# A's scores scaled and reduced by one VectorE operation, and an order computed with a shared port

## The chip, the cores and the metric

The kernel runs on one core of a Trainium2 chip. The metric is the device time of one execution in microseconds (us), and the median of several executions where more are there. TensorE is PE in the profile (its weight loads are PEld), VectorE is DVE, ScalarE is ACT, GpSimd is POOL, and SyncE, which issues most DMAs, is SP.

## The reference

Two layers over 512 latent tokens and 256 context tokens of width 1024. Each layer normalises and modulates its input, projects it once, and attends in three groups of eight heads of 64:

```python
hx = rmsnorm(x, norm_w) * (1 + scale[:, None, :]) + shift[:, None, :]
px = split_cols(hx @ w_in); pc = split_cols(hc @ w_in)
ya, yca = global_gqa(...)            # A: every latent query reads all 512 latent and 256 context keys
yb, ycb = neighbourhood_attn(...)    # B: a window of 8 x 16 grid cells with a learned bias, and all context keys
yc_, ycc = window_gqa(...)           # C: +-128 tokens with a sink logit, and all context keys
ux = jnp.concatenate([ya, yb, yc_], axis=-1) * jax.nn.silu(px[9])
x = x + gate[:, None, :] * (ux @ w_out)
```

In A, queries and keys are RMS-normalised per head before the rotary turn, so a row of A's scores carries a factor that belongs to its query: `softmax(r * s)`, with one `r` for each query and head. The context tokens attend to the context alone, in the first layer only. A final RMSNorm ends the kernel.

## The kernel before

Everything is float32, and each product is taken as three products of rounded halves (`hh`, `hl`, `wh`, `wl`), which is why TensorE has so much to do. The attention of a layer goes by pairs of heads: four pairs of B, then A and C in turn (A0, C0, A1, C1, ..., A3, C3). While one pair attends, TensorE also projects q, k, v and gates of pairs to come; under the last pair (C3) it starts the output projection instead (`head`, L512), and the projected rows that this reads are reloaded and split just ahead of use (`reload`, `split_u`, L484 and L485).

A pair is cut into units. A unit of A (`GlobalUnit`) is one head and two tiles of 128 queries; its scores, 768 columns a tile, fill the three PSUM banks of `Sbig`, so tile 0 ends and tile 1 begins in the middle bank. A `CtxUnit` (layer 0) is the 256 context queries of one head, 256 columns for each of two tiles. For each tile of A three steps follow: VectorE takes the negated maximum of the raw scores out of PSUM (L1167), multiplies it by `r` (L1169, one element a row), and ScalarE computes `exp(r * s - max)` from PSUM into a tile `P` in SBUF, with `r` as its scale (L1171). A DMA on SP's queue then copies `P` to a tile `R5` or `R2`, shown as R (`ship`, L1052), so that `P` may be used anew; there are two buffers of `P`, for all units of A, B and C. TensorE turns R into a bank `T` (L1057), ScalarE rounds it to `pth` (L785), VectorE keeps the rest in `ptl` (L1037), and TensorE multiplies both with the values into `Obig` (L1041). Units of C and B do it otherwise: one VectorE operation adds a mask or bias to the scores, writes them to `P` in SBUF, and finds their extreme (L1219, L1279, a `tensor_tensor_reduce`; the trace calls it CUSTOM_DVE_ANT_0, the order ISA), and ScalarE's exponential works in place on `P` (L1222, L1281).

What sets the order is `arrange`: once the program is written, a model of the five engines, the DMA queues and the buffers (`Step.cost`, `Graph.run`) plays it several times with ranks from the pass before, and the best order is fixed, engine by engine, by added dependencies. Engines run their instructions strictly in that order. [...] So a change of one cost can move instructions anywhere.

Of the kernel before, what the change touches and what calls it, by code (L numbers as in the profile page):

```python
# [12 lines left out]
F32 = mybir.dt.float32  # L13
F32R = mybir.dt.float32r
BF16 = mybir.dt.bfloat16
AF = mybir.ActivationFunctionType
OP = mybir.AluOpType
AX = mybir.AxisListType
# [32 lines left out]
CFG = dict(hp=600, hpf=600, pj=2, T=2, O=1, P=2, R5=5, R2=2, qt=5, kt=4, vt=4, gt=3, wh=5, ws=3, pt=3, bm=2, tA=1, OT=1, u=1, tl=1, turns=6, ab="pj", tR=1, map={}, ada=2, h0=300, h1=1000, a0=9, H=2, hr=0, cp="A", cv="A", w0="D", w1="D", w2=(("D", "D"), ("D", "D")), hb="D", ws_="P")  # L51
# [14 lines left out]
def body(tc, xT, small, bcast, rpb, adaw, adat, wt, wf, wo, trigA, trigQ, trigC, mskB, mskC, outT):  # L66
    nc = tc.nc
    es = ExitStack()
    const = es.enter_context(tc.tile_pool(name="const", bufs=1))
# [6 lines left out]
    ident = const.tile([128, 128], F32)  # L76
# [8 lines left out]
    nc.vector.memset(ones, 1.0)  # L85
    mhalf = const.tile([128, 8], F32)
    nc.vector.memset(mhalf, -0.5)
    onesw = const.tile([128, 64], F32)
    nc.vector.memset(onesw, 1.0)
    onepair = const.tile([128, 2], F32)  # L90
    nc.vector.memset(onepair, 0.0)
    for h in range(2):
# [363 lines left out]
    udram = {}  # L456
# [302 lines left out]
def mixers(tc, nc, l, last, p1, ps, const, env):  # L759
    g_ = env  # L760
    en = g_["en"]
    (pj, Sbig, psT, psO, half_O, opv, after, ADA, wlo, proj_f, proj_t, ada, ada_load, ident, identr, bc, sm, pairs, onesw, mhalf, negsink, udram, dram, hpool, rpb,
     trigA, trigQ, trigC, mskB, mskC) = [g_[k] for k in (
         "pj", "Sbig", "psT", "psO", "half_O", "opv", "after", "ADA", "wlo", "proj_f", "proj_t", "ada", "ada_load", "ident", "identr", "bc", "sm", "pairs", "onesw", "mhalf",
         "negsink", "udram", "dram", "hpool", "rpb", "trigA", "trigQ", "trigC", "mskB", "mskC")]
    nq = 4 if last else 6
    ncol = nq * 128
# [335 lines left out]
    def ahead(steps):  # L1103
# [10 lines left out]
        late[0](late[1])  # L1114
        yield late[2]

    class CtxUnit(Unit):
        def scores(self):
            S = Sbig[:, 0:512]
            for t in range(2):  # L1120
                for x in range(2):
                    mul(S[:, t * 256:(t + 1) * 256], self.Q[:, NT + t * 128:NT + (t + 1) * 128],
                                     self.K[:, x, NT:NA], start=(t == 0 and x == 0), stop=(x == 1),
                                     skip_group_check=True)
            nm = self.stat("negm", 4, 2)
            nc.vector.tensor_reduce(nm, S[:, 0:512].rearrange("p (t c) -> p t c", t=2), axis=AX.X, op=OP.max,
                                    negate=True)
            if self.sink is not None:
                nc.vector.tensor_scalar(nm, nm, self.sink, None, op0=OP.min)
            rs = self.c["rs"]  # L1130
            if rs is not None:
                nc.vector.tensor_mul(nm, nm, rs[:, 4:6, self.h])
            P = newP()
            for t in range(2):
                nc.scalar.activation(P[:, t * 256:(t + 1) * 256], S[:, t * 256:(t + 1) * 256], AF.Exp,
                                     bias=self.stat("negm", 4 + t), accum_out=self.stat("sums", 4 + t),
                                     **({} if rs is None else dict(scale=rs[:, 4 + t, self.h:self.h + 1])))
            self.P = ship(P, 512)
            yield 0.45

# [13 lines left out]
    class GlobalUnit(Unit):  # L1154
        def scores(self):
            self.P = []
            for i in self.tiles:
                cx, loc = ((512, 0), (768, 1024))[i % 2]
                for c0, c1, o in ((NT, NA, cx), (0, NT, loc)):
                    for x in range(2):  # L1160
                        mul(Sbig[:, o:o + c1 - c0], self.Q[:, i * 128:(i + 1) * 128],
                                         self.K[:, x, c0:c1], start=(x == 0), stop=(x == 1), skip_group_check=True)
                yield 0.65
            for i in self.tiles:
                S = Sbig[:, 768 * (i % 2):768 * (i % 2) + 768]
                nm = self.stat("negm", i)
                nc.vector.tensor_reduce(nm, S, axis=AX.X, op=OP.max, negate=True)  # L1167
                r = self.c["rs"][:, i, self.h:self.h + 1]
                nc.vector.tensor_mul(nm, nm, r)  # L1169
                P = newP()  # L1170
                nc.scalar.activation(P, S, AF.Exp, bias=nm, scale=r, accum_out=self.stat("sums", i))  # L1171
                self.P.append(ship(P, 768, ((512, 768), (0, 256))[i % 2]))
                yield 0

# [403 lines left out]
    def urgent(gen):  # L1578
        while True:
# [10 lines left out]
ENGINES = {"PE": "PE", "Activation": "ACT", "DVE": "DVE", "Pool": "POOL", "SP": "SP"}  # L1590
CAPS = dict(x0=8, ada=9, x1=8, sq=3, rstd=3, pj=CFG["pj"], ws=CFG["ws"], wh=CFG["wh"], wl=CFG["wh"], hL=16, hC=16,
            T=CFG["T"], spr=2, nw=1, P=CFG["P"], R5=CFG["R5"], R2=CFG["R2"], qt=CFG["qt"], kt=CFG["kt"], vt=CFG["vt"], gt=CFG["gt"], negm=2,
            bm=CFG["bm"], sums=2, pth=CFG["pt"], ptl=CFG["pt"], rec=2, ssA=2, qd=2, rs=3, ex=2, xr=3, xn0=8, room=9,
            xn1=8, rbl=2)
POOLS = ("p0_", "p1_0_", "p2_0_", "p1_1_", "p2_1_")
BANKS = ("pj", "T", "Sbig", "Obig")
# [11 lines left out]
def size(ap):  # L1608
    n = 1
    for _, c in ap[1:]:  # L1610
        n *= c
    return n


class Step:
# [16 lines left out]
    def cost(self, tiles):  # L1632
        ins = [u for u in self.use if not u[1]]
        outs = [u for u in self.use if u[1]]
        n = max([size(u[2]) for u in ins + outs[:1]] or [0])
        bank = any(stem(u[0].name) in BANKS for u in ins)
        op = str(getattr(self.inst, "op", getattr(self.inst, "func", ""))).split(".")[-1]
        e = self.engine
        self.plain, self.turn, self.switch = False, None, 0.0
        if self.dma:  # L1640
            b = 4 * outs[0][2][0][1] * size(outs[0][2])
            out = stem(outs[0][0].name).split("_")[0]
            far = any(u[0].name not in tiles or tiles[u[0].name][1] for u in ins)
            self.busy = ISSUE.get(out, 430.0)
            self.fixed = 2400.0 if far else 1650.0
            self.move = 3460.0 if out == "bc" else b / (340.0 if far else 395.0)
        elif e == "PE":
            n = size(ins[0][2])
            exact = ins[0][4] == "float32"
            self.turn = outs[0][0].name if stem(ins[0][0].name) in ("ident", "identr") and n == 128 else None  # L1650
            self.switch = 5.0 if exact else 86.0
            self.busy = {128: 108.0, 256: 57.0, 2: 112.0}[n] if exact else n / 2.4 + (13.5 if n > 128 else 12.0)
            self.last = 272.0 if exact else n / 2.4 + 180.0
        else:
            if e == "ACT":
                d = 172.0 + 0.83 * n + (0 if bank else 35)
            elif e == "DVE":
                d = 156.0 + 0.52 * n if self.kind == "InstTensorCopy" and not bank else 152.0 + 1.06 * n
                self.plain = self.kind == "InstTensorTensor" and not bank and n >= 256
            elif op == "pow":  # L1660
                d = 1000.0
            elif self.kind == "InstTensorScalarPtr":
                d = 440.0 + 2.2 * n if n > 8 else 190.0
            else:
                d = 190.0 + 2.14 * n if n > 64 else 150.0
            self.busy = max(d - BEHIND[e], 20.0)
            self.last = d
            if e == "ACT" and op == "Exp" and n > 12:
                self.busy, self.last = d - 16, d + 91
# [18 lines left out]
class Graph:  # L1688
# [76 lines left out]
    def run(self, rank):  # L1765
# [14 lines left out]
        for t, v in self.order.items():  # L1780
            if self.pool[t] is not None:
                stage_left[self.pool[t]] += len(v)
        lanes, ring, data = [], {}, {}
        prev, row, done = None, 0, 0

        def push(k):
# [10 lines left out]
        while done < n:  # L1797
# [42 lines left out]
            if s.dma:  # L1840
                begin = max(t + s.fixed, ring.get(e, 0.0))
                fin = begin + s.move
                for x, (a, b) in data.items():
                    if x != e:
                        fin += 0.5 * max(0.0, min(b, fin) - max(a, begin))
                ring[e], data[e] = fin, (fin - s.move, fin)
                lanes.append(fin)
                fin += TO_LAND
            elif e == "PE":
                fin = t + s.last  # L1850
                if not s.turn and prev is not None and prev.turn:
                    busy += prev.switch
                    fin += prev.switch
                row = row + 1 if s.turn else 0
                if row > 2 and s.switch > 5:
                    busy += 20
                if t < SLOW:
                    busy *= 2
                    fin += s.last
                prev = s  # L1860
            else:
                extra = 0.55 * min(free["POOL"] - t, s.last) if s.plain and free["POOL"] > t else 0.0
                fin = t + s.last + extra
                busy += extra
            free[e] = t + busy
# [194 lines left out]
```

## Time and profile before

| | |
|---|---|
| three executions | 1184.32, 1188.16, 1190.93 us; median 1188.16 |
| the profiled execution | 1184.9 us, span 1183.1 us, granted TensorE clock 0.989 |
| PE | busy 1121.9 us, 95% of the span (ends of matmuls are modelled) |
| DVE, ACT, POOL | 789.7 us (67%), 689.4 us (58%), 409.8 us (35%) |
| attention of A and C | about 240 to 600 us in layer 0, about 840 to 1125 us in layer 1 |

A row of a group names line, engine, operation, tiles and shapes, the count, then busy time and mean time of one. A row of waits names who waited for whom, the total in us, how often, and the longest. In a timeline, the bracket is the idle time of the engine before the row and what ended it. In a table of stretches, the last three columns are the granted TensorE clock, the share of DMA time and GB/s.

### The profile page before, as it was taken

How to read it: one execution, taken by the hardware profiler on the slowest of the kernel's cores; microseconds unless marked ns; L12 is line 12 of the kernel's file. 1: busy time of each engine (PE TensorE's matmuls, PEld its weight loads, DVE VectorE, ACT ScalarE, POOL GpSimd, SP SyncE). 2: the span in 40 equal slices, each digit the busy share in tenths (PEclk: the TensorE clock that was granted, in tenths of full speed). 3: DMA queues.
4: the chain of work that ended last, by engine and by line, in shares of the span. 5: the costliest groups of instructions: out<-in, count | busy, mean ns of one | idle time of the engine just before them, and what ended most of it. 6: DMA issues, size and time to landing. Idle time of an engine off the chain costs nothing. (4 is left out here: it accounts for less than half of the span.)

```text
span 1183.1 us, 21230 instructions
## 1 busy us (share of the span) xinstructions
PE 1121.9 (95%) x7352; PEld 977.3 (83%) x7352; DVE 789.7 (67%) x1548; ACT 689.4 (58%) x1466; POOL 409.8 (35%) x364
## 2 busy tenths in 40 slices
PE   5999899999999999998789999999999999999996
PEld 3798888997878888887678989988987888887776
DVE  6666667655565668669879765678557566758653
ACT  5445555565666667777632544565566677677551
POOL 2430202155454365536200012121166655475001
PEclk9999999999999999999899999999999999999998
DMA  9555435435465455456758542565344444566352
GB/s 344 182 165 163 148 124 189 147 126 160 154 194 169 155 176 187 134 173 212 215 175 318 176 152 78 166 195 170 110 157 161 157 165 166 169 182 203 133 170 72
DMA packets 111540, 200.95 MB, mean 170 GB/s; under 512 B 13676, under 2 KB 32456, under 8 KB 111432
## 3 DMA queue, kind: packets, MB, share of 16 engines
q1 hardware_dynamic: 103440, 184.01, 48.0%
q10 hardware_dynamic: 7992, 15.58, 4.1%
q8 instruction: 58, 0.95, 0.3%
q14 instruction: 50, 0.41, 0.1%
HBM read 116.46 MB, written 11.25 MB: 108 GB/s over the span
## 5 line engine op out<-in xcount | busy, mean ns | idle before, releaser
L315 PE MATMUL pj<-hL,wh 128*128 128x512 f32 x880 | 294.0, 401 | 1.4 <-DVE rs L889 0.9
L1037 DVE TENSOR_TENSOR ptl<-T,pth 128x512 fp32r<-128x512 f32 (+1 forms) x264 | 172.0, 668 | 55.1 <-ACT pth L785 50.1
L785 ACT ACTIVATE pth<-T 128x512 fp32r<-128x512 f32 (+1 forms) x264 | 147.3, 584 | 88.9 <-PE T L1057 75.4
L315 PEld LDWEIGHTS pj<-hL,wh 128*128 128x128 f32 x880 | 159.8, 188 | 30.6 <-issue 2.6
L315 PE MATMUL pj<-hL,wl 128*128 128x512 f32 x440 | 174.8, 398 | 0.0
L249 ACT ACTIVATE wh<-ws 128x512 fp32r<-128x512 f32 x192 | 119.7, 630 | 78.1 <-PE pj L315 33.7
L1041 PE MATMUL Sbig<-kt,qt 128*128 128x256 f32 (+1 forms) x864 | 154.3, 307 | 6.7 <-DVE negm L1219 3.0
L252 POOL TENSOR_TENSOR wl<-ws,wh 128x512 fp32r<-128x512 f32 x76 | 99.7, 1314 | 148.0 <-ACT wh L249 110.5
L1057 PEld LDWEIGHTS T<-identr,R 128*128 128x128 f32 x1024 | 105.6, 141 | 50.0 <-DVE ptl L1037 18.9
L1041 PEld LDWEIGHTS Sbig<-kt,qt 128*128 128x128 f32 x864 | 126.8, 190 | 19.8 <-DVE negm L1219 5.0
L1057 PE MATMUL T<-identr,R 128*128 128x128 f32 x1024 | 116.4, 245 | 25.7 <-DMA R<-P 13.4
L1041 PE MATMUL Obig<-pth,vt 128*128 128x256 f32 (+2 forms) x432 | 126.9, 310 | 1.2 <-ACT pth L785 0.5
L1041 PE MATMUL Obig<-ptl,vt 128*128 128x256 f32 (+2 forms) x432 | 125.7, 309 | 1.2 <-DVE ptl L1037 1.2
L252 DVE TENSOR_TENSOR wl<-ws,wh 128x512 fp32r<-128x512 f32 x116 | 83.5, 729 | 32.0 <-ACT wh L249 22.1
L315 PE MATMUL pj<-hC,wh 128*128 128x256 f32 x512 | 100.5, 286 | 0.1
L315 PEld LDWEIGHTS pj<-hL,wl 128*128 128x128 f32 x440 | 82.9, 188 | 13.9 <-issue 0.4
L1041 PEld LDWEIGHTS Obig<-pth,vt 128*128 128x128 f32 x432 | 82.1, 190 | 9.7 <-ACT pth L785 2.0
L1041 PEld LDWEIGHTS Obig<-ptl,vt 128*128 128x128 f32 x432 | 81.8, 189 | 6.8 <-DVE ptl L1037 2.1
L1171 ACT ACTIVATE P<-Sbig,negm,rs 128x768 f32<-128x768 f32 x64 | 63.4, 991 | 37.7 <-DVE negm L1169 22.8
L315 PEld LDWEIGHTS pj<-hC,wh 128*128 128x128 f32 x512 | 82.2, 191 | 1.9 <-issue 0.3
L1167 DVE TENSOR_REDUCE negm<-Sbig 128x1 f32<-128x768 f32 x64 | 61.0, 954 | 33.4 <-ACT P L1171 21.6
L315 PE MATMUL pj<-hC,wl 128*128 128x256 f32 x256 | 73.3, 286 | 0.0
(345 smaller groups left out, 2287.8 us busy)
## 6 DMA issues: line engine op xcount, KB each, us to landing
R<-P SPq DMA_DIRECT2D x216, 256.0 KB
ws<-wf_dram SPq DMA_DIRECT2D x120, 256.0 KB
ada<-adaw_dram SPq DMA_DIRECT2D x32, 512.0 KB
ws<-wo_dram SPq DMA_DIRECT2D x57, 256.0 KB
bm<-mskB_dram SPq DMA_DIRECT2D x16, 576.0 KB
R<-P SPq DMA_DIRECT2D x64, 128.0 KB
ws<-wt_dram SPq DMA_DIRECT2D x24, 256.0 KB
tB<-tA SPq DMA_DIRECT2D x72, 64.0 KB
```

The source lines that it names most:

```text
L249: nc.scalar.activation(hi, src, AF.Copy)
L252: eng.tensor_sub(lo, src, hi.bitcast(F32))
L315: nc.tensor.matmul(p[:, 0:n], a[:, r, :], cols(b[kt], c0, n), start=(i == 0), stop=(i == 23))
L785: nc.scalar.activation(out, src, AF.Copy)
L1037: nc.vector.tensor_sub(lo[:, 0:n], T[:, 0:n], hi[:, 0:n].bitcast(F32))
L1041: return nc.tensor.matmul(*args, **kw)
L1057: return nc.tensor.transpose(out.bitcast(F32R), src, identr)
L1167: nc.vector.tensor_reduce(nm, S, axis=AX.X, op=OP.max, negate=True)
L1171: nc.scalar.activation(P, S, AF.Exp, bias=nm, scale=r, accum_out=self.stat("sums", i))
```

## The change

There are two parts. The first concerns units of A alone. A new function `scaled` has VectorE read the scores from PSUM, multiply them by `r` (broadcast along the row), write the products to `P` in SBUF and leave their maximum in `m`, in one `tensor_tensor_reduce` of full width. A one-element `tensor_reduce` negates `m`, and the exponential works in place on `P`, without a scale. `P` is thus taken by VectorE, and the scores' banks in `Sbig` are read for the last time by VectorE. A's context units do this once for each tile, where one reduction covered both.

The second part changes the model that computes the order. The flag `plain`, which was for VectorE's wide tensor-tensor operations on SBUF, becomes `port`, on both engines: on VectorE for all tensor-tensor, tensor-scalar and copy operations that read no PSUM, and others with two wide inputs; on GpSimd for everything with an input. Each is slowed by 0.6 of what is left of the other engine's port operation. GpSimd's `pow` costs 385 + 158 n ns, where it was 1000, and DMAs that spread the reciprocal sums out of DRAM (`u`) are taken to need 3 us more. An unused tile of ones goes.

```diff
+    def scaled(unit, i, S, P):
+        n = S.shape[-1]
+        nm = unit.stat("negm", i)
+        r = unit.c["rs"][:, i, unit.h:unit.h + 1]
+        m = p1.tile([128, 1], F32, name="m", bufs=2)
+        nc.vector.tensor_tensor_reduce(out=P, in0=S, in1=r.to_broadcast([128, n]), op0=OP.mult, op1=OP.max, scale=1.0,
+                                       scalar=-3.0e38, accum_out=m)
+        nc.vector.tensor_reduce(nm, m, axis=AX.X, op=OP.max, negate=True)
+        nc.scalar.activation(P, P, AF.Exp, bias=nm, accum_out=unit.stat("sums", i))
...
     class GlobalUnit(Unit):
...
                 S = Sbig[:, 768 * (i % 2):768 * (i % 2) + 768]
-                nm = self.stat("negm", i)
-                nc.vector.tensor_reduce(nm, S, axis=AX.X, op=OP.max, negate=True)
-                r = self.c["rs"][:, i, self.h:self.h + 1]
-                nc.vector.tensor_mul(nm, nm, r)
                 P = newP()
-                nc.scalar.activation(P, S, AF.Exp, bias=nm, scale=r, accum_out=self.stat("sums", i))
+                scaled(self, i, S, P)
...
-                self.plain = self.kind == "InstTensorTensor" and not bank and n >= 256
+                big = [u for u in ins if size(u[2]) == n]
+                self.port = not bank and (self.kind in ("InstTensorTensor", "InstTensorScalarPtr", "InstTensorCopy")
+                                          or len(big) > 1)
             elif op == "pow":
-                d = 1000.0
+                d = 385.0 + 158.0 * n
+                self.port = True
...
+            if out == "u" and far:
+                self.fixed += 3000.0
...
-                extra = 0.55 * min(free["POOL"] - t, s.last) if s.plain and free["POOL"] > t else 0.0
+                extra = 0.0
+                if s.port:
+                    extra = 0.6 * max(port.get("POOL" if e == "DVE" else "DVE", t) - t, 0.0)
+                    port[e] = t + s.last + extra
```

The order of all engines comes out anew. Three places follow; lines of the changed kernel are two lower up to the new function and five higher behind it (L1035 is L1037 before, L1224 is L1219). First VectorE in the first two units of A in layer 0, before:

```order
L1167 TENSOR_REDUCE negm<-Sbig 128x1
L1169 TENSOR_TENSOR negm<-negm,rs 128x1
L1167 TENSOR_REDUCE negm<-Sbig 128x1
L1375 SCALAR_TENSOR_TENSOR OT<-OT,u 128x512
L1169 TENSOR_TENSOR negm<-negm,rs 128x1
L1375 SCALAR_TENSOR_TENSOR OT<-OT,u 128x256
L209 MEMSET pj 128x256
L223 COPY adasb<-pj 128x256
L1167 TENSOR_REDUCE negm<-Sbig 128x1
L1169 TENSOR_TENSOR negm<-negm,rs 128x1
```

And VectorE at the same place after (the second ISA row of a pair reads the extreme out into `m`):

```order
L1121 ISA P,m<-Sbig,rs 128x768
L1121 ISA m 128x1
L1121 ISA P,m<-Sbig,rs 128x768
L1121 ISA m 128x1
L1123 TENSOR_REDUCE negm<-m 128x1 x2
L1363 COPY rT<-T 12x128
L1075 TENSOR_TENSOR OT<-Obig,OT 64x256
L1121 ISA P,m<-Sbig,rs 128x768
L1121 ISA m 128x1
L207 MEMSET pj 128x256
```

Both tiles of a unit now pass VectorE before the first negated maximum is made, so both banks' reads are over before the first exponential may start.

Second, TensorE under the second head of C3 in layer 0, from that head's last scores (Sbig<-kt,qt) on; R_7070 is a context tile, and rows of `pj` from L512 (L510 after) are the output projection. Before:

```order
L1041 MATMUL Sbig<-kt,qt 128x256 x6
L1041 MATMUL Obig<-ptl,vt 128x256
L1041 MATMUL Obig<-pth,vt 128x256
L1041 MATMUL Obig<-ptl,vt 128x256
L1041 MATMUL Obig<-pth,vt 128x384
L1041 MATMUL Obig<-ptl,vt 128x384
L1041 MATMUL Obig<-pth,vt 128x384
L1057 MATMUL T<-identr,R_7070 128x128 x4
L512 MATMUL pj<-qt,wh 128x512
L512 MATMUL pj<-qt,wl 128x512
L1041 MATMUL Obig<-ptl,vt 128x384
L512 MATMUL pj<-qt,wh 128x512
```

And TensorE there after:

```order
L1039 MATMUL Sbig<-kt,qt 128x256 x5
L1039 MATMUL Obig<-ptl,vt 128x256
L1039 MATMUL Obig<-pth,vt 128x384
L1055 MATMUL T<-identr,R_7132 128x128 x4
L1039 MATMUL Obig<-ptl,vt 128x384
L1039 MATMUL Obig<-pth,vt 128x384
L510 MATMUL pj<-kt,wh 128x512 x3
L510 MATMUL pj<-kt,wl 128x512
L1039 MATMUL Obig<-ptl,vt 128x384
L510 MATMUL pj<-ut,wh 128x512 x2
L510 MATMUL pj<-ut,wl 128x512
L510 MATMUL pj<-kt,wh 128x512
```

Output projection stood ahead of these scores and stands behind them now: from the last scores to the first turn of that head's own R there are 4 matmuls of 512 columns before and 18 after.

Third, VectorE under the first head of C3 in layer 0, where one of the reloaded rows is split (kt<-uf). Before:

```order
L1219 ISA P,negm<-Sbig,msk,negsink 128x640
L1219 ISA negm 128x1
L1358 COPY rT<-T 12x128
L1037 TENSOR_TENSOR ptl<-T,pth 128x512
L1077 TENSOR_TENSOR OT<-Obig,OT 64x256
L1219 ISA P,negm<-Sbig,msk,negsink 128x512
L1219 ISA negm 128x1
L485 TENSOR_TENSOR kt<-uf,kt 128x768
L1219 ISA P,negm<-Sbig,msk,negsink 128x512
L1219 ISA negm 128x1
L1077 TENSOR_TENSOR OT<-Obig,OT 64x256
L1126 TENSOR_REDUCE negm<-Sbig 128x2
```

The split is made under the second head of C3 after, again on VectorE:

```order
L1224 ISA P,negm<-Sbig,msk,negsink 128x640
L1224 ISA negm 128x1
L1035 TENSOR_TENSOR ptl<-T,pth 128x512
L1380 SCALAR_TENSOR_TENSOR OT<-OT,u 128x256
L1035 TENSOR_TENSOR ptl<-T,pth 128x384
L483 TENSOR_TENSOR kt<-uf,kt 128x768
L1035 TENSOR_TENSOR ptl<-T,pth 128x384
L1224 ISA P,negm<-Sbig,msk,negsink 128x512
L1224 ISA negm 128x1
L1035 TENSOR_TENSOR ptl<-T,pth 128x512
L156 ISA junk_8477,mod_2_107<-dots,sm 128x512
L156 ISA mod_2_107 128x1
```

The split stood behind the operation that takes the third buffer of `P` of its head, and stands ahead of it now.

More of the change, by code (lines that the diff above doesn't have):

```diff
@@ L87, in body @@
     nc.vector.memset(mhalf, -0.5)
-    onesw = const.tile([128, 64], F32)
-    nc.vector.memset(onesw, 1.0)
     onepair = const.tile([128, 2], F32)
@@ L761, in mixers @@
     en = g_["en"]
-    (pj, Sbig, psT, psO, half_O, opv, after, ADA, wlo, proj_f, proj_t, ada, ada_load, ident, identr, bc, sm, pairs, onesw, mhalf, negsink, udram, dram, hpool, rpb,
+    (pj, Sbig, psT, psO, half_O, opv, after, ADA, wlo, proj_f, proj_t, ada, ada_load, ident, identr, bc, sm, pairs, mhalf, negsink, udram, dram, hpool, rpb,
      trigA, trigQ, trigC, mskB, mskC) = [g_[k] for k in (
-         "pj", "Sbig", "psT", "psO", "half_O", "opv", "after", "ADA", "wlo", "proj_f", "proj_t", "ada", "ada_load", "ident", "identr", "bc", "sm", "pairs", "onesw", "mhalf",
+         "pj", "Sbig", "psT", "psO", "half_O", "opv", "after", "ADA", "wlo", "proj_f", "proj_t", "ada", "ada_load", "ident", "identr", "bc", "sm", "pairs", "mhalf",
          "negsink", "udram", "dram", "hpool", "rpb", "trigA", "trigQ", "trigC", "mskB", "mskC")]
@@ L1124, in scores @@
                                      skip_group_check=True)
[L1125 to L1132, printed above, removed]
-            P = newP()
[L1134 to L1137, printed above, removed]
+            P = newP()
+            if self.c["rs"] is not None:
+                for t in range(2):
+                    scaled(self, 4 + t, S[:, t * 256:(t + 1) * 256], P[:, t * 256:(t + 1) * 256])
+            else:
+                nm = self.stat("negm", 4, 2)
+                nc.vector.tensor_reduce(nm, S[:, 0:512].rearrange("p (t c) -> p t c", t=2), axis=AX.X, op=OP.max,
+                                        negate=True)
+                if self.sink is not None:
+                    nc.vector.tensor_scalar(nm, nm, self.sink, None, op0=OP.min)
+                for t in range(2):
+                    nc.scalar.activation(P[:, t * 256:(t + 1) * 256], S[:, t * 256:(t + 1) * 256], AF.Exp,
+                                         bias=self.stat("negm", 4 + t), accum_out=self.stat("sums", 4 + t))
             self.P = ship(P, 512)
@@ L1592 @@
             T=CFG["T"], spr=2, nw=1, P=CFG["P"], R5=CFG["R5"], R2=CFG["R2"], qt=CFG["qt"], kt=CFG["kt"], vt=CFG["vt"], gt=CFG["gt"], negm=2,
-            bm=CFG["bm"], sums=2, pth=CFG["pt"], ptl=CFG["pt"], rec=2, ssA=2, qd=2, rs=3, ex=2, xr=3, xn0=8, room=9,
+            bm=CFG["bm"], sums=2, pth=CFG["pt"], ptl=CFG["pt"], rec=2, ssA=2, qd=2, rs=3, m=2, ex=2, xr=3, xn0=8, room=9,
             xn1=8, rbl=2)
@@ L1638, in cost @@
         e = self.engine
-        self.plain, self.turn, self.switch = False, None, 0.0
+        self.port, self.turn, self.switch = False, None, 0.0
         if self.dma:
@@ L1658, in cost @@
                 d = 156.0 + 0.52 * n if self.kind == "InstTensorCopy" and not bank else 152.0 + 1.06 * n
-                self.plain = self.kind == "InstTensorTensor" and not bank and n >= 256
+                big = [u for u in ins if size(u[2]) == n]
+                self.port = not bank and (self.kind in ("InstTensorTensor", "InstTensorScalarPtr", "InstTensorCopy")
+                                          or len(big) > 1)
             elif op == "pow":
-                d = 1000.0
+                d = 385.0 + 158.0 * n
+                self.port = True
             elif self.kind == "InstTensorScalarPtr":
+                self.port = True
                 d = 440.0 + 2.2 * n if n > 8 else 190.0
             else:
+                self.port = bool(ins)
                 d = 190.0 + 2.14 * n if n > 64 else 150.0
@@ L1782, in run @@
                 stage_left[self.pool[t]] += len(v)
-        lanes, ring, data = [], {}, {}
+        lanes, ring, data, port = [], {}, {}, {}
         prev, row, done = None, 0, 0
```

## The prediction

> **What bounds the kernel.** I read the engines' shares, then who waits for whom in stages, then the stretches and the timeline around the worst waits, then the durations. TensorE is the bound:
>
> ```profile
> PE 1121.9 (95%) x7352; PEld 977.3 (83%) x7352; DVE 789.7 (67%) x1548; ACT 689.4 (58%) x1466; POOL 409.8 (35%) x364
> ```
>
> Its work does not change, so only its waits and its clock can. TensorE's waits (total in us, times, longest) from 60 to 240 us (B of layer 0, the first row), from 240 to 540 (A and C of layer 0, two rows), from 540 to 600 (the end of that attention, five), and from 840 to 1130 (layer 1, the two largest):
>
> ```profile
> PE T L1057 <- DMA R<-P: 2.0, 1, 2.0
> ...
> PE T L1057 <- DVE ptl L1037: 2.6, 3, 1.4
> PE Sbig L1041 <- ACT P L1171: 1.3, 2, 0.9
> ...
> PE T L1057 <- DMA R<-P: 5.9, 2, 3.2
> PE T L1057 <- DVE ptl L1037: 2.0, 2, 1.2
> PE pj L512 <- DVE kt L485: 1.9, 1, 1.9
> PE Sbig L1041 <- DVE negm L1219: 1.1, 1, 1.1
> PE Sbig L1041 <- ACT P L1135: 0.9, 1, 0.9
> ...
> PE T L1057 <- DVE ptl L1037: 5.1, 7, 1.7
> PE T L1057 <- DMA R<-P: 3.8, 6, 1.7
> ```
>
> So 60 us at the end of layer 0's attention hold 11.8 us of waits, more than the two large rows of layer 1's 290 us, and there the clock falls too (third column from the right):
>
> ```profile
> 566.00:578.00 12.00, 7.48 (x44) 5.88 (x42) 7.23 (x19) 4.96 (x12) 1.16 (x1) 0.99 0.84 229
> 578.00:590.00 12.00, 10.70 (x56) 9.11 (x57) 11.93 (x28) 8.26 (x18) 4.64 (x3) 0.72 0.56 182
> 590.00:602.00 12.00, 8.71 (x43) 7.19 (x44) 9.98 (x25) 5.14 (x15) 0.00 (x0) 0.86 0.77 264
> ```
>
> The timeline shows how these waits arise:
>
> ```profile
> 570.71 0.75 DVE L1219 CUSTOM_DVE_ANT_0 P<-Sbig,msk,negsink 128x512 f32<-128x512 f32 x1 [2.08 <-DMA R<-P]
> 571.39 0.08 DVE L1219 DVE_READ_ACCUMULATOR2_ANT negm<- 128x1 f32 x1
> 571.39 0.95 DVE L485 TENSOR_TENSOR kt<-uf,kt 128x768 fp32r<-128x768 f32 x1
> ...
> 574.13 0.39 PE L512 MATMUL pj<-kt,wh 128*128 128x512 f32 x1
> 574.36 0.39 PE L512 MATMUL pj<-kt,wl 128*128 128x512 f32 x1
> 578.17 1.55 PE L1057 MATMUL T<-identr,R 128*128 128x128 f32 x8 [2.75 <-DMA R<-P]
> ...
> 590.94 0.28 PE L1041 MATMUL Obig<-pth,vt 128*128 128x256 f32 x1
> 591.05 0.28 PE L1041 MATMUL Obig<-ptl,vt 128*128 128x256 f32 x1
> 594.49 1.43 PE L1057 MATMUL T<-identr,R 128*128 128x128 f32 x8 [3.16 <-DMA R<-P]
> ```
>
> VectorE waited for a buffer of `P` that a DMA still read; the split of `kt`, which needs none, stood behind it. TensorE had too little to do between C3's scores and its turns. Matmuls start 0.23 us apart at 512 columns and 0.11 at 256; with these spacings I count the order's work below.
>
> **The change, part by part.** The operations of A first, by shape, then the fixed parts:
>
> ```profile
> L1171 ACT ACTIVATE P<-Sbig,negm,rs 128x768 f32<-128x768 f32 x64 | 63.4, 991 | 37.7 <-DVE negm L1169 22.8 <-PE pj L315 4.8 <-issue 4.3
> L1167 DVE TENSOR_REDUCE negm<-Sbig 128x1 f32<-128x768 f32 x64 | 61.0, 954 | 33.4 <-ACT P L1171 21.6 <-PE Sbig L1041 11.4
> L1169 DVE TENSOR_TENSOR negm<-negm,rs 128x1 f32<-128x1 f32 x64 | 26.7, 417 | 1.1
> L1279 DVE CUSTOM_DVE_ANT_0 P<-Sbig,bm 128x512 f32<-128x512 f32 x32 | 22.0, 688 | 14.3 <-PE Sbig L1041 4.4 <-DMA R<-P 3.9 <-POOL bm L1460 2.8
> L1279 DVE CUSTOM_DVE_ANT_0 P<-Sbig,bm 128x448 f32<-128x448 f32 x32 | 19.8, 618 | 11.9 <-PE Sbig L1041 5.8 <-DMA R<-P 5.7
> L1222 ACT ACTIVATE P<-P,negm 128x640 f32<-128x640 f32 x32 | 26.5, 827 | 11.5 <-DVE negm L1219 4.9 <-issue 3.2 <-DVE sums L1343 2.5
> L1222 ACT ACTIVATION_READ_ACCUMULATOR P<-P,negm 128x1 f32 x64 | 12.1, 189 | 0.0
> L1135 ACT ACTIVATE P<-Sbig,negm,rs 128x256 f32<-128x256 f32 x16 | 8.9, 560 | 7.0 <-DVE negm L1132 2.7 <-issue 2.4 <-PE pj L315 1.1
> L1135 ACT ACTIVATE P<-Sbig,negm 128x256 f32<-128x256 f32 x32 | 14.9, 470 | 10.0 <-DMA R<-P 3.7 <-DVE negm L1126 3.5 <-DVE negm L1129 2.5
> ...
> L228 DVE TENSOR_REDUCE mod<-pj x16: 146/152/168, 281.7 to 501.5; 128x2 f32<-128x8 f32 x16
> L1169 DVE TENSOR_TENSOR negm<-negm,rs x64: 142/159/1615, 272.2 to 1091.5; 128x1 f32<-128x1 f32 x64
> ```
>
> *VectorE.* Removed: 64 x (954 + 417) ns = 87.7 us. The 417 is a mean; the median is 159 and the longest 1615, for one element a row: this operation at times waits for something else, while the small reduction below never took more than 168. Added: the fused operation at 768 columns, by L1279's slope of 70 ns for 64 columns 688 + 280 = 968; its readout 80; a small reduction, nearest L228, 152. 64 x 1200 = 76.8 us, 11 less. The eight context units of A pay two operations where they had one, some 0.1 us each way, nothing. Removed too are 21.6 us in which VectorE's second maximum waited for the first exponential: the tiles share a bank.
>
> *ScalarE.* From SBUF at 768 columns: 827 + 128 x 0.83 = 933 ns against 991, 64 x 58 = 3.7 us less on an engine busy 58%: nothing by itself. The scale operand alone costs 560 - 470 = 90 ns. [...]
>
> *A unit's chain and the banks:*
>
> ```profile
> 442.49 0.96 DVE L1167 TENSOR_REDUCE negm<-Sbig 128x1 f32<-128x768 f32 x1 [1.52 <-PE Sbig L1041]
> 447.07 1.00 ACT L1171 ACTIVATE P<-Sbig,negm,rs 128x768 f32<-128x768 f32 x1 [0.45 <-DVE negm L1169]
> ...
> 918.03 3.88 DMA R<-P
> 1104.26 3.34 DMA R<-P
> ```
>
> From the first maximum to the second exponential's end are 5.6 us here. Now: twice the fused operation and its readout, 1.05, two reductions, 0.3, and twice the exponential and its readout, 1.1, make 4.6, and the banks are free after 2.1. TensorE's waits for A's exponentials are 1.3 + 0.9 us in the rows above: **-2.0** (0 to -2.2). Of the 9.7 us of waits for `ptl` (2.6 + 2.0 + 5.1) I take a quarter, since 32 of VectorE's 790 us, 11 of work and 21 of waiting, no longer stand ahead of them: **-2.5** (0 to -9.7; what could make them longer is the next part).
>
> *The `P` buffers.* Against this, VectorE takes `P` now, 2.4 us before the exponential does. The chain of what ended last has ten DMAs R<-P, the first and the last of them above; they take 2.05 to 4.86 us, mean 3.7. A buffer was held 1.0 + 0.1 + 3.7 = 4.8 us, and will be 7.1. A pair of A in layer 1 needs eight through two buffers: 28.4 us. In the new order the scores of pairs A1, A2 and A3 there leave 26.1, 25.6 and 27.0 us of TensorE work to the first scores of C, some 27.4 with the 5% of the span in which PE is not busy, so each pair lacks 1 us; layer 0's pairs, with 34.7 us of work on average (36.4 so stretched) for eight tiles and two smaller ones held 5.6 us, lack nothing: **+3** (0 to +17, with buffers held 8.3 us). What queues behind such a wait is `ptl`, and then TensorE's next turn.
>
> *End of layer 0's attention.* From the first C3 head's last scores to its first turn the order has 5.1 us of TensorE work before and 10.5 after, in the second head 3.2 and 6.2. Of 2.75 and 3.16 us of wait 0 and 0.2 are left: **-5.7**, with bounds of 0 (DMAs run at 0.84 there) and -5.9. The split of `kt` now stands ahead of the wait for `P`: **-1.5** (0 to -1.9). The clock lost 0.28 x 12 + 0.14 x 12 = 5.0 us of full-speed time; I take half, **-2.5** (0 to -5.0). [...]
>
> *The rest.* C3 of layer 1 gets 1 us more work between scores and turns: **-1** of the 3.8 (0 to -1.7). One unit of B gets 0.6 us less where it now waits 2.0: **+0.6**. New costs and the shared port's wider term re-deal all other rows: 0, within 3 either way.
>
> Sum: -2.0 - 2.5 + 3 - 5.7 - 1.5 - 2.5 - 1 + 0.6 = -11.6. The profiled execution took 1184.9, so 1173.3; the median of the three runs lies 3.3 above it, so **1177 us**.
>
> **The rivals.**
>
> *The end stays as it is.* R<-P is late there because DMAs are busy, and new cover only moves the wait. Then 9.7 of the gain goes, and the time is 1186. For it: 229 GB/s and 0.84 in that stretch; against it: the wait is counted from work that ran out.
>
> *Buffers of `P` bind (slower).* If R<-P takes 4.9 us, as the longest of the chain, `P` is held 8.3 us. Layer 1 lacks 33.2 - 27.4 = 5.8 us in each of three pairs; layer 0's pairs need (8 x 8.3 + 2 x 6.8) / 2 = 40.0 and lack 3.6. That is 28 where I have 3: 1202 us. It decides from about 7.8 us held, where layer 1 lacks 3 x 3.8 and layer 0 3 x 1.1, 14.7 in all, and nothing is left of the gain. For it, C's operations wait for `P` already:
>
> ```profile
> DVE P L1219 <- DMA R<-P: 17.4, 14, 3.6
> ```
>
> Against it: these are 14 of C's 64 operations, 1.2 us each, and not all of them held TensorE up.
>
> *The order is re-dealt for the worse.* The port term charges operations whose contention the trace hardly shows, and 4 us of new waits come in B, at the start or in the output projection: 1181.
>
> *More goes.* All waits for `ptl`, all the lost clock, no lack of `P`: 1164.
>
> **How the numbers follow.** Forecast 0.50 (its own range 1170 to 1183), the end stays 0.20, buffers bind 0.12, re-dealt 0.10, more 0.08. Half a per cent, 5.9 us, is about what a measurement here can tell from no change; so faster means under 1182. Faster: 0.45 + 0.03 + 0.05 + 0.08 = 0.61, rounded to 0.62; within: 0.27; slower, nearly all from the buffers: 0.11. The range, 1166 to 1192, leaves out the far ends of the last and of the buffers' case.
>
> **What would show it.** Right: groups of A at 970, 80, 150 and 930 ns; TensorE's waits at the end of layer 0's attention under 4 us in all, and the clock at 1.0 there; no wait for A's exponentials. Wrong: VectorE waiting for R<-P at the fused operation by more than 20 us in all, with more waits for `ptl` behind it; or the same two waits at C3; or new waits in B.

## The result and the profile after

The changed kernel takes 1150.85 us (median of four runs, 1149.40 to 1151.87), the kernel before 1188.81 beside it: a ratio of 0.9685, 95% interval 0.9653 to 0.9716. That is 38 us less, where the forecast was 11 less, and 15 us below the range. The profiled execution has a span of 1150.0 us (1183.1 before) and a granted clock of 0.996 (0.989). The engines' row of the page after:

```profile
PE 1106.9 (96%) x7352; PEld 973.1 (85%) x7352; DVE 771.2 (67%) x1643; ACT 684.2 (59%) x1466; POOL 412.0 (36%) x364
```

TensorE has the same 7352 matmuls, and yet it is busy for 15.0 us less. Only the other 18.1 of the 33.1 us of span are idle time (1183.1 - 1121.9 before, 1150.0 - 1106.9 after). The clock explains about 8 of the 15: 0.011 x 1183 = 13.0 us lost before, 0.004 x 1150 = 4.6 after, if the loss falls where TensorE is busy. The other 7 lie within what the page counts as busy.

TensorE's waits after (waited for, us in total, times, longest), from 60 to 240 us, from 240 to 540 (two rows), 540 to 600 (three) and 840 to 1130 (two):

```profile
PE T L1055 <- DMA R<-P: 1.1, 1, 1.1
...
PE T L1055 <- DMA R<-P: 2.2, 2, 1.2
...
PE T L1055 <- DVE ptl L1035: 0.2, 1, 0.2
...
PE Sbig L1039 <- ACT P L1145: 1.3, 1, 1.3
PE T L1055 <- DVE ptl L1035: 1.2, 1, 1.2
PE T L1055 <- DMA R<-P: 0.7, 1, 0.7
...
PE T L1055 <- DMA R<-P: 2.4, 4, 1.4
PE Sbig L1039 <- DVE negm L1224: 0.5, 1, 0.5
```

The turns' waits for `ptl`, 2.6, 2.0 and 5.1 us before in the last three of these windows, are 0.2, 1.2 and none at L1055 (two other turns, at L1058, wait 0.4 us each). All the waits in the lists of the four windows add up to 36.4 us before and 17.0 after. At the end of layer 0's attention the two long waits for R<-P are gone, and with them the loss of clock (stretches of the changed kernel; third column from the right):

```profile
548.00:560.00 12.00, 9.14 (x51) 6.66 (x50) 7.51 (x17) 7.00 (x17) 4.64 (x3) 1.00 0.89 278
560.00:572.00 12.00, 10.71 (x64) 9.17 (x63) 11.86 (x29) 8.29 (x20) 2.59 (x2) 1.00 0.52 177
572.00:584.00 12.00, 11.20 (x65) 8.86 (x64) 8.78 (x21) 3.03 (x6) 0.00 (x0) 1.00 0.62 194
```

The operations of A after (groups by shape), and last VectorE's wait for a buffer of `P` at the fused operation over the whole span:

```profile
L1121 DVE CUSTOM_DVE_ANT_0 P<-Sbig,rs 128x768 f32<-128x768 f32 x64 | 60.4, 951 | 30.5 <-DMA R<-P 16.7 <-PE Sbig L1039 10.5 <-PE pj L215 1.8
L1121 DVE DVE_READ_ACCUMULATOR2_ANT m<- 128x1 f32 x80 | 6.5, 82 | 0.0
L1123 DVE TENSOR_REDUCE negm<-m 128x1 f32<-128x1 f32 x80 | 11.4, 147 | 0.7
L1124 ACT ACTIVATE P<-P,negm 128x768 f32<-128x768 f32 x64 | 59.7, 933 | 20.0 <-DVE negm L1123 12.0 <-issue 4.5 <-ACT P L1124 1.0
...
DVE P L1121 <- DMA R<-P: 16.7, 12, 3.5
```

The 21.6 us in which VectorE waited for an exponential have no row any more. 16.7 us of waiting for DMAs are new at this place, and its idle time there is 30.5 us where the old maximum had 33.4.

Where did the time come from? Undisturbed, matmuls start 0.228 us apart at 512 columns, 0.174 at 384, 0.119 at 256 and 0.072 for a turn in these traces (the few of other shapes are counted as 256). Taking from each gap what is beyond this (if over 25 ns; slow clock, waits and short stalls together) gives the time lost between starts: 110.5 us before and 79.1 after, nearly all of the difference. By stage, cut where the first operation on the scores of a stage starts, with the stages of A and C ending at C's last operation on its scores (the stretches before and behind these four lose 18.5 us in both):

| time lost, us | B of layer 0 | A and C of layer 0 | up to A of layer 1 | A and C of layer 1 |
|---|---|---|---|---|
| before | 10.8 | 44.7 | 11.6 | 24.9 |
| after | 7.2 | 25.3 | 11.2 | 16.8 |

Of 31 us, 27 lie in the stages of A and C, and they lie all over them. The end of layer 0's attention, on which 9.7 us of my sum's 11.6 stood, is the smaller part: from C3's first scores to behind its last turns (563 to 602 us before, 534 to 584 after, a little beyond the table's cut) the loss fell from 15.4 to 8.8 us. Ahead of C3 it fell by 14 us in layer 0.

### The profile page after: what moved, and what is told of

It reads as the page before. It is cut to its first block, busy times and chain, and to the rows that moved or that the text cites. A ratio compares the mean times of both kernels' runs of the same rounds, so it can differ in the third digit from the quotient of the medians.

```text
span 1150.0 us, 21370 instructions
## 1 busy us (share of the span) xinstructions
PE 1106.9 (96%) x7352; PEld 973.1 (85%) x7352; DVE 771.2 (67%) x1643; ACT 684.2 (59%) x1466; POOL 412.0 (36%) x364
## 4 chain that ended last, share of the span: by engine, by line
PE 75%; DMA 9%; DVE 8%; issue 3%; ACT 3%; POOL 1%; SPq 0%; ACTq 0%; DVEq 0%; POOLq 0%
PE pj L313 30%; PE Sbig L1039 8%; PE Obig L1039 8%; PE T L1055 6%; DMA R<-P 5%; PE pj L334 5%; PE pj L510 3%; PE T L510 3%; PE Sbig L510 2%; PE T L313 2%; DVE junk L156 2%; PE Sbig L421 1%; DMA x<-xT_dram 1%; DMA uf<-u 1%; PE Sbig L334 1%
## 5 line engine op out<-in xcount | busy, mean ns | idle before, releaser
L1035 DVE TENSOR_TENSOR ptl<-T,pth 128x512 fp32r<-128x512 f32 (+1 forms) x264 | 172.7, 670 | 80.3 <-ACT pth L783 76.1
L1055 PEld LDWEIGHTS T<-identr,R 128*128 128x128 f32 x1024 | 106.0, 140 | 27.3 <-DMA R<-P 7.5
L1055 PE MATMUL T<-identr,R 128*128 128x128 f32 x1024 | 113.7, 242 | 8.6 <-DMA R<-P 6.3
L1121 DVE CUSTOM_DVE_ANT_0 P<-Sbig,rs 128x768 f32<-128x768 f32 (+1 forms) x80 | 66.6, 845 | 31.9 <-DMA R<-P 16.7
L1124 ACT ACTIVATE P<-P,negm 128x768 f32<-128x768 f32 (+1 forms) x80 | 67.7, 847 | 22.9 <-DVE negm L1123 13.9
L1465 POOL TENSOR_TENSOR bm<-wr,bm 128x192 f32<-128x192 f32 (+1 forms) x48 | 40.0, 861 | 95.1 <-DMA bm<-mskB_dram 46.7
```

The source lines that it names most:

```text
L1035: nc.vector.tensor_sub(lo[:, 0:n], T[:, 0:n], hi[:, 0:n].bitcast(F32))
L1055: return nc.tensor.transpose(out.bitcast(F32R), src, identr)
L1121: nc.vector.tensor_tensor_reduce(out=P, in0=S, in1=r.to_broadcast([128, n]), op0=OP.mult, op1=OP.max, scale=1.0, scalar=-3.0e38, accum_out=m)
L1124: nc.scalar.activation(P, P, AF.Exp, bias=nm, accum_out=unit.stat("sums", i))
L1465: nc.gpsimd.tensor_add(b, src, b)
```

## Experiments

The rivals after the result: theory W, VectorE's work and its coupling to ScalarE in A are what went; theory M, the corrected costs find a better order; theory L, any new order moves the time this much. "With the old model" means `Step.cost` and `Graph.run` as they were before. A time stands against the kernel before on the same chip, in brackets the 95% interval.

**The two parts apart, and the order dealt anew.** e1 is the changed kernel with the old model, e2 the kernel before with the changed model. e3 and e4 are the kernels before and after with one unrelated cost moved:

```diff
-TO_PE, TO_OTHER, TO_LAND = 400.0, 150.0, 700.0
+TO_PE, TO_OTHER, TO_LAND = 410.0, 150.0, 700.0
```

> The changed operations of A, with the order's model as it was before (plain, 0.55, pow 1000, no 3 us on u). Theory W (VectorE's work and its coupling to ScalarE in A are what went: 87.7 us of reductions and products became some 75, and 21.6 us of waiting for the first exponential are gone, so ptl comes in time everywhere): most of the 38 us is here, 1150 to 1160 us, ptl waits of TensorE under 4 us. Theory M (the gain is the better order that the corrected costs find): 1172 to 1190 us. Theory L (any new dealing of the order moves the time by 10 us or more): anything, and the two re-dealt kernels beside it show the same spread.

> A's operations as they were before, with the changed model of the order (port term on both engines, pow 385 + 158 n, 3 us more on u). Theory W: 1180 to 1190 us, TensorE's waits for ptl still 8 us or more. Theory M: 1155 to 1170 us. Theory L: differs from the kernel before by as much as the re-dealt kernels do.

> The kernel before, with one cost of the model that has nothing to do with the change moved by 10 ns (an engine's result reaches TensorE after 410 ns instead of 400). This deals the whole order anew. Theories W and M: within 6 us of 1188. Theory L: 10 us or more away.

> The changed kernel with the same 10 ns in the model. Theories W and M: within 6 us of 1151. Theory L: 10 us or more away, most likely slower, since the changed kernel would have been a lucky deal.

| | median us | ratio |
|---|---|---|
| e1, fused operation alone | 1161.53 | 0.979 (0.976 to 0.982) |
| e2, model alone | 1172.64 | 0.989 (0.985 to 0.992) |
| e3, before with a new order | 1186.93 | 1.000 (0.999 to 1.002) |
| e4, after with a new order | 1159.75 | 0.978 (0.975 to 0.980) |

The parts' 25 and 13 us add up to the whole. But e4 gives back 9 us for nothing but a new order: on the scale of single parts theory L cannot be left out, and from here on one order is not taken as proof of 10 us. e2 keeps the coupling and the wait for it (VectorE's waits in e2, over the span), and e3 has a lesson of its own (TensorE's waits in e3 from 540 to 600 us):

```profile
DVE negm L1167 <- ACT P L1171: 20.4, 24, 1.4
...
PE Sbig L512 <- ACT P L1135: 3.4, 1, 3.4
PE Sbig L1041 <- DVE mod L158: 3.1, 1, 3.1
PE T L1057 <- DVE ptl L1037: 1.7, 1, 1.7
```

e3's waits for R<-P at the end of layer 0's attention are gone too (5.9 us before), and it is no faster: the waits shown, 8.2 us, have come in the same 60 us.

**What of the fused operation?** e5 keeps the old operations and the old model, and only changes the program order in a unit: both maxima and products, then both exponentials, so that the second maximum does not wait for the first exponential.

```diff
             for i in self.tiles:
...
                 nc.vector.tensor_mul(nm, nm, r)
+            for i in self.tiles:
...
                 P = newP()
                 nc.scalar.activation(P, S, AF.Exp, bias=nm, scale=r, accum_out=self.stat("sums", i))
```

> The kernel before, its model too; only the program order of a unit of A changes: both tiles' maximum and product first, then both exponentials, so that the second maximum no longer waits for the first exponential (21.6 us of VectorE's waiting before). Both exponentials then wait for the second maximum instead. If this coupling is most of what the fused operation removed (1186 to 1161 with the old model): 1165 to 1175 us. If VectorE's work or the port is it: 1183 to 1190 us.

e6 makes the product by another operation, to take the stalls away:

```diff
-                nc.vector.tensor_mul(nm, nm, r)
+                nc.vector.tensor_tensor_reduce(out=m[:, 0:1], in0=nm, in1=r, op0=OP.mult, op1=OP.max, scale=1.0,
+                                               scalar=-3.0e38, accum_out=m[:, 1:2])
```

> The kernel before, its model too; the one-element product (mean 417 ns, up to 1615) is made by a one-element tensor_tensor_reduce, an operation that did not show the wait for GpSimd, at some 150 ns and a readout of 80. VectorE's 26.7 us there become some 15. If the port stalls are most of the fused operation's gain: 1165 to 1175 us. If the coupling of the two tiles is: 1182 to 1190 us.

e7 and e8 are the changed kernel in its own order, with the model's costs of the altered operation held as they were:

```diff
-        nc.vector.tensor_reduce(nm, m, axis=AX.X, op=OP.max, negate=True)
+        nc.vector.tensor_reduce(nm, m.to_broadcast([128, 180]), axis=AX.X, op=OP.max, negate=True)   # e7
+        nc.vector.tensor_scalar(nm, m, -1.0, None, op0=OP.mult)                                      # e8
```

> The changed kernel with the changed kernel's order on every engine, row for row; the small reduction that negates the maximum reads its element 180 times, so it takes some 190 ns more (147 to about 340), 80 times: 15 us more of VectorE's work, about what the change took away. If VectorE's work in A is what the gain is: 1159 to 1166 us (8 to 15 more). If it is the coupling or the order: under 4 us more, 1150 to 1155.

> The changed kernel with its order of tiles on every engine; the negation is a one-element tensor_scalar on SBUF, the kind that waits for GpSimd, in place of the reduction that does not. If such stalls are what the gain is: the negation's mean goes from 147 ns to some 400 and the time up by 8 us or more, beyond e7. If not: under 4 us more.

| | median us | ratio |
|---|---|---|
| e5, two loops | 1168.16 | 0.982 (0.980 to 0.985) |
| e6, product by another operation | 1189.40 | 1.000 (0.998 to 1.002) |
| e7, 190 ns more a tile | 1152.89 | 0.970 (0.967 to 0.972) |
| e8, negation by tensor_scalar | 1151.11 | 0.968 (0.966 to 0.970) |

e5 gains 21 us without the fused operation, by the order of two loops. VectorE's row at the maximum, in e5, has no wait for the exponential any more:

```profile
L1167 DVE TENSOR_REDUCE negm<-Sbig 128x1 f32<-128x768 f32 x64 | 58.2, 947 | 15.9 <-PE Sbig L1041 15.8
L1169 DVE TENSOR_TENSOR negm<-negm,rs 128x1 f32<-128x1 f32 x64 | 25.1, 398 | 0.2
```

The product is as slow as it was (398 ns against 417). e7 shows that VectorE's work is not the point once the wait is gone: the group of L1123 took 25.8 us instead of 11.4, and the time is within the interval of the changed kernel. e6 did not take the stalls away, so it says nothing on them (what they need is told at the end); 5 us more of readouts, in an order dealt anew, cost nothing that shows. e8 had no stalls: its negation took 148 ns (median), not the 400 that I expected.

The timeline of the kernel before shows how the coupling holds TensorE up, in the last pair of A in layer 1 (VectorE, ScalarE, then TensorE):

```profile
1077.41 0.96 DVE L1167 TENSOR_REDUCE negm<-Sbig 128x1 f32<-128x768 f32 x1 [0.20 <-PE Sbig L1041]
1078.29 1.22 DVE L485 TENSOR_TENSOR hL<-uf,hL 128x512 fp32r<-128x512 f32 x1
1079.43 1.23 DVE L1169 TENSOR_TENSOR negm<-negm,rs 128x1 f32<-128x1 f32 x1
1080.59 0.68 DVE L1375 SCALAR_TENSOR_TENSOR OT<-OT,u 128x512 f32<-128x512 f32 x1
1081.86 0.96 DVE L1167 TENSOR_REDUCE negm<-Sbig 128x1 f32<-128x768 f32 x1 [0.60 <-ACT P L1171]
1082.74 0.68 DVE L1037 TENSOR_TENSOR ptl<-T,pth 128x512 fp32r<-128x512 f32 x1
...
1080.75 0.99 ACT L1171 ACTIVATE P<-Sbig,negm,rs 128x768 f32<-128x768 f32 x1 [1.42 <-DVE negm L1169]
1081.64 0.19 ACT L1171 ACTIVATION_READ_ACCUMULATOR P<-Sbig,negm,rs 128x1 f32 x1
1081.73 1.07 ACT L785 ACTIVATE pth<-T 128x512 fp32r<-128x512 f32 x2
...
1083.47 0.54 PE L1057 MATMUL T<-identr,R 128*128 128x128 f32 x4 [1.69 <-DVE ptl L1037]
```

The product stalls (1.23 us for one element a row); ScalarE idles 1.42 us for it; the second maximum waits for that exponential; behind the maximum stands `ptl`, behind the exponential stands `pth`, which `ptl` needs, and TensorE's next turn waits 1.69 us for `ptl`. Each engine keeps its order, so a wait on the one is handed to the other and back.

**The coupling put back, and crossed with the model.** e9 is e1 with a read by ScalarE of one score in the shared middle bank after each exponential, e10 is e5 with the changed model, e11 and e12 are e5 and e2 with the 10 ns of e3.

```diff
         nc.scalar.activation(P, P, AF.Exp, bias=nm, accum_out=unit.stat("sums", i))
+        if n > 256:
+            x = 512 if i % 2 == 0 else 0
+            nc.scalar.activation(m, S[:, x:x + 1], AF.Copy)
```

> e1 (the fused operation, the old model; 1161.5) with the coupling put back: after each exponential of a full tile ScalarE reads one score of the tile in the middle bank, so the second tile's fused operation must wait for the first tile's exponential again, as the maximum did. ScalarE has some 64 x 0.2 = 13 us more to do, at 59% busy. If the coupling is the cause: 1180 to 1195 us, and VectorE waits for ScalarE at the fused operation by 20 us or more. If e1 was faster for another reason: 1158 to 1166.

> e5 (old operations in two loops) with the changed model of the order. If the coupling and the model are all there is, this comes to within 8 us of the changed kernel: 1150 to 1160 us, and the fused operation is not needed. If the fused operation itself (less work, banks free earlier) is worth something beyond: 1163 to 1170.

> e5 with the 10 ns of e3 in the model, to see how far e5's 1168 is luck of the order. Coupling: 1160 to 1176 us. Luck: 1180 or more.

> e2 (the changed model alone, 1172.6) with the 10 ns of e3. If the model's costs are worth 13 us in earnest: 1167 to 1178 us. If e2 was a lucky order: 1180 to 1190.

| | median us | ratio |
|---|---|---|
| e9, fused operation, coupled | 1171.56 | 0.986 (0.984 to 0.989) |
| e10, two loops, changed model | 1161.38 | 0.978 (0.975 to 0.982) |
| e11, two loops, new order | 1171.19 | 0.987 (0.985 to 0.990) |
| e12, model alone, new order | 1177.41 | 0.991 (0.989 to 0.994) |

Put back, the coupling costs 9 us against e1, fewer than the 19 or more I expected, and VectorE's wait for it is 4.7 us, not 20 (last entry of the row):

```profile
L1121 DVE CUSTOM_DVE_ANT_0 P<-Sbig,rs 128x768 f32<-128x768 f32 x64 | 60.9, 952 | 27.4 <-PE Sbig L1039 11.8 <-DMA R<-P 6.7 <-ACT m L1127 4.7
```

The read itself is 10.7 us more work for ScalarE and holds the scores' banks longer (TensorE waits for it once, 1.8 us), so the 9 us are not the coupling's alone. The order, computed with the coupling in view, puts other work between the two tiles: the second fused operation starts 2.7 us after the first (mean of 32 units; 2.0 in e1). So by this run the coupling is at most a part of the fused operation's gain. Two loops hold their gain in a new order (15 us in e11, 21 in e5), the model alone too (11 and 13). With e10 the old operations come within some 11 us of the changed kernel, and are as fast as e4, the same change in another order.

**The product, and the model's three edits.** In e13 ScalarE makes the product of the full tiles, all else as before. e14, e15 and e16 undo one edit of the model each in the changed kernel (the 3 us on `u`, `pow`'s cost, the port term).

```diff
-                nc.vector.tensor_mul(nm, nm, r)
+                nc.scalar.activation(nm, nm, AF.Copy, scale=r)
```

> The kernel before, its model too; the one-element product of each full tile goes from VectorE to ScalarE (64 x some 0.2 us there), so VectorE is rid of 26.7 us and of the stalls in this chain, while the second maximum still waits for the first exponential. If the product's stalls in the coupled chain cost TensorE's time (which would explain the 16 us of e9): 1170 to 1178 us. If only the coupling does: 1184 to 1192.

> The changed kernel without the 3 us more on the DMAs of u. If these are what the model gives: 1158 to 1164 us. If the port term or pow is: 1148 to 1155. A new order alone moved the changed kernel by 9 us (e4), so less than that says nothing by itself.

> The changed kernel with pow at 1000 ns in the model again. If the cost of pow is what the model gives: 1158 to 1164 us. If not: 1148 to 1155.

> The changed kernel with the narrow port term of before (plain, 0.55, VectorE alone). If the wider port term is what the model gives: 1158 to 1164 us. If not: 1148 to 1155.

| | median us | ratio |
|---|---|---|
| e13, product on ScalarE | 1174.72 | 0.987 (0.984 to 0.990) |
| e14, no 3 us on `u` | 1159.69 | 0.974 (0.971 to 0.978) |
| e15, `pow` at 1000 ns | 1157.21 | 0.972 (0.969 to 0.976) |
| e16, old port term | 1162.24 | 0.976 (0.973 to 0.979) |

e13 still has the coupling, 24.5 us of it, and gains 15 us all the same:

```profile
L1167 DVE TENSOR_REDUCE negm<-Sbig 128x1 f32<-128x768 f32 x64 | 61.2, 956 | 47.2 <-ACT P L1171 24.5 <-PE Sbig L1041 22.6
```

So the product on VectorE seems to be the other half of that chain, as e9 had suggested: to take away either link frees most of the time, and the fused operation, which takes away both (e1), gives 25 us and not the sum of the two. e13 was not dealt a second time, and it takes away the product's work together with its stalls; which of the two counts stays open. Each of the model's edits seems to be worth 4 to 9 us when undone; that is no more than e4's new order, so none of them is shown to matter by itself.

**Is the changed kernel's own order a lucky one?** e17 is e1 with the 10 ns of e3, e18 the changed kernel with 390 ns.

> e1 (the fused operation, old model, 1161.5) with the 10 ns of e3. If the model's costs are worth some 10 us with the fused operation too: 1162 to 1172 us, above all orders with the changed model. If the changed kernel's order is luck: 1151 to 1161, among them.

> The changed kernel with 390 ns where it has 400 (e4 had 410). If the changed model gives 1151 in earnest: 1147 to 1155 us. If that was a lucky order: 1156 to 1163.

e17 takes 1166.00 us, 0.979 (0.976 to 0.982), and e18 1161.12, 0.975 (0.972 to 0.978). All the runs by what they hold, as ratios:

| | old model | changed model |
|---|---|---|
| old operations | 1, e3 1.000 | e2 0.989, e12 0.991 |
| old operations in two loops | e5 0.982, e11 0.987 | e10 0.978 |
| fused operation | e1 0.979, e17 0.979 | changed kernel 0.9685, e4 0.978, e18 0.975 |

Read down, decoupling gains in both columns and in every order, whether by two loops or by the fused operation. What the fused operation gives beyond two loops is less sure: 0.3 to 0.8% with the old model, and with the changed one nothing in e4, 0.3% in e18 and 1% in the changed kernel. Read across, the model is worth some 1% with the old operations and 0.4 to 0.9% with two loops; with the fused one, 0.1 to 0.4% in e4 and e18 and 1% in the changed kernel. So of its 38 us some 8 to 11 come with the order it happened to get, against two others of the same costs. Whether orders as good are rare, three cannot tell. No run was faster than the changed kernel beyond its interval.

## Why the prediction was wrong

The direction and nearly all mechanisms were right; two terms were far too small.

*Waits for `ptl`, -2.5, a quarter of 9.7.* This is the step that failed. I had seen both links (21.6 us of VectorE's waiting, a product that stalls for up to 1615 ns), and priced them by the waits that TensorE's list puts down to `ptl`. Those fell by 8.3 of 9.7 us, already beyond my quarter, and 2.0 us more in B, which I had left out, went as well. (The 21 us of waiting that I counted among VectorE's 790 us are not in them: 790 is its busy time.) But the list of waits holds less than half of what TensorE loses: 36 us are listed in the four windows of the prediction, and 80 us are lost between starts in those stages (10.8 + 44.7 + 24.9). Of the 80, some 41 us stand at starts behind a listed wait, and 40 at 437 starts behind none, under 0.4 us each, slow clock among them; these fell by 22 and 9, where my terms for waits sum to 9 and my term for the clock was 2.5. So most of what I missed was listed, but under other names than `ptl`; that those waits come from the same late engines fits, and no run shows it wait by wait. The rival "more goes", 1164, was the nearest, and too small for the same reason: it too ended at the waits for `ptl` and the clock. The runs put 15 to 21 us on the coupling (e11, e5), 15 on the product (e13), and 25 on the fused operation with all it does (e1, e17), where I had 4.5 for it without the buffers' +3.

*The new order, "0, within 3 either way".* Orders with the same costs lie 8 to 11 us apart (e4, e18), and the model's costs gave 11 to 13 us with the old operations. A gain of the model's was not in my sum.

*Durations.* Fused operation, readout and reduction: 951 + 82 + 147 against the 968 + 80 + 152 I took; exponential 933, as worked out. The time from the first maximum to the end of the second exponential, 5.6 and 4.6 us by my one example, is 6.1 and 5.25 as a mean of 32 units.

*A's exponentials, -2.0.* Right: no wait for them is left, and 0.9 us for L1121 stand in their place.

*Buffers of `P`, +3.* They were held for 7.0 us on average (7.1 by my working), and VectorE waited for them at the fused operation for 16.7 us, 9.4 of it in layer 1, in reach of the 20 I had named. It hardly reached TensorE: waits for R<-P in layer 1 went from 3.8 to 2.4 us, and those for `ptl` there from 5.1 to 0.4. The mechanism was there and cost about nothing, probably because VectorE now has time to wait; no run tests that.

*End of layer 0's attention, -5.7, -1.5 and -2.5.* Waits for R<-P there went from 5.9 to 0.7, the wait for `kt` from 1.9 to none, and the clock is at 1.00, the whole 5.0 and not half. Right as an account of that place, and the rival that it stays so is out, even at a DMA share of 0.89 (548 to 560 us). But e3 shows that taking such a wait away is not yet a gain.

*Clock.* In the kernel before, the granted clock was 0.72 from 578 to 590 us, behind the wait of 2.75 us. In the kernel after it fell behind a shorter one too: a wait of 1.44 us is followed by the only slow stretch of layer 1's attention (0.80 and 0.63 from 1044 to 1050 us).

```profile
1045.41 0.44 PE L1055 MATMUL T<-identr,R 128*128 128x128 f32 x3 [1.44 <-DMA R<-P]
...
1044.00:1047.00 3.00, 1.58 (x6) 1.31 (x7) 1.47 (x3) 2.42 (x5) 1.17 (x1) 0.80 0.58 194
1047.00:1050.00 3.00, 3.00 (x14) 2.65 (x13) 2.70 (x4) 1.47 (x3) 2.92 (x3) 0.63 0.75 251
1050.00:1053.00 3.00, 2.96 (x22) 2.51 (x21) 2.27 (x4) 2.32 (x6) 2.35 (x3) 1.00 0.94 276
```

*C3 of layer 1, -1, and B, +0.6.* The time lost in C3 fell from 3.4 to 1.0 us. B lost 10.8 us before, 7.2 after, and 12.0 in e18: luck of the order, with the wrong sign in my sum.

## What to carry to other kernels

When two engines in fixed order wait for each other within one unit (here: maximum, product, exponential, then the next maximum on a shared bank), taking that dependence away can be worth more than the bound engine's list says for the one wait in which you see it (here 15 to 21 us in e11 and e5, against 9.7 of listed waits for `ptl`): compare the spacing of its starts with the undisturbed spacing before you cap a gain by listed waits. Breaking any one link, even by the order of two loops in the program, may bring most of it (those 15 to 21 us, of the fused operation's 25). And where a solver deals the order, run two or three neighbours of a kernel before you credit an edit with less than the spread between them, here 10 us.

## What the runs showed of the hardware

In these runs operations on VectorE of one or two elements a row stalled at times where they read two operands from SBUF, whatever the operation is called: up to 1615 ns in the kernel before, 1622 in e6 and 1344 in the kernel after, against 158 at most in e8, where they read one. The product of e6 (a tensor_tensor_reduce, two operands), the negation of e8 (a tensor_scalar with one operand and a constant) and the tensor_scalar with a column as its second operand in the kernel after (two elements a row; ns, shortest, median, longest):

```profile
L1170 DVE CUSTOM_DVE_ANT_0 m<-negm,rs x64: 140/160/1622, 271.1 to 1094.0; 128x1 f32<-128x1 f32 x64
...
L1123 DVE TENSOR_SCALAR negm<-m x80: 131/148/158, 267.1 to 1056.1; 128x1 f32<-128x1 f32 x80
...
L1143 DVE TENSOR_SCALAR negm<-negm,negsink x8: 211/226/1344, 330.6 to 568.2; 128x2 f32<-128x2 f32 x8
```

The fused operation also has two operands, but one in PSUM, and never took more than 960 ns. I had taken the kind of operation for the cause. In the kernel before, the product took 153 ns on average where GpSimd was idle (35 times) and 737 where an operation of GpSimd ran beside it (29 times); in all but one of the 29 it ended 12 to 25 ns after that operation. Of e8's 80 negations 43 started while an operation of GpSimd ran, and none took more than 158 ns. So the product waited for GpSimd, and the negation, with one operand, did not; that a port is what the two engines share, as the model's term assumes, no run shows.

The slow clock after the 1.44 us above cost TensorE about as much again as the wait itself: 0.20 x 3 + 0.37 x 3 = 1.7 us of full-speed time in the two stretches. The length of a wait alone does not decide it: the wait of 1.9 us for `kt` in the kernel before, which ended at 572 us, was followed by none (0.99 from 566 to 578).
